# A two-layer decoder trunk: own places for each activation form, another row order in the last two output tiles, and two interleaved pairs

## The chip, the cores and the metric

The kernel runs on one core of a Trainium2 chip. TensorE (PE) does the matrix products, ScalarE (ACT) and VectorE (DVE) split, scale and gate, GpSimd (POOL) does small jobs and issues the accumulating loads, SyncE (SP) issues all other DMAs. The metric is the device time of one execution in microseconds, as the median of several runs.

## The reference, cut to what matters

512 positions, 2048 channels, two layers and a final norm, all in float32:

```python
def shortconv_layer(h, w_in, conv_w, w_out):
    gate_b, gate_c, u, z = jnp.split(h @ w_in, 4, axis=-1)
    y = gate_b * causal_depthwise_conv(gate_c * u, conv_w)
    return (y * jax.nn.silu(z)) @ w_out

def reference(...):
    h = x
    h = h + hybrid_layer(rmsnorm(h, norm_w[0]), ...)     # DeltaNet and windowed attention heads
    h = h + shortconv_layer(rmsnorm(h, norm_w[1]), ...)  # w_in: 2048 x 12288, w_out: 3072 x 2048
    return rmsnorm(h, final_norm_w)
```

The hybrid layer ends in an output projection of 3072 rows (24 tiles of 128, called rows 0 to 23 here) to 2048 columns (16 tiles). Its sum with x is h1, which the second layer normalizes, projects and gates.

## The kernel before

Activations stand with channels on the 128 partitions and the 512 positions along the free axis. Every float32 operand is split into a high and a low part, `hi` (a rounded copy, made by ACT) and `lo` (the difference, made by DVE), and each product is three matmuls: hi x hi, hi x lo, lo x hi (`mm3`). Weights come from DRAM in blocks of 128 x 8 x 128 (512 KB) and are split the same way (`load_split`, `split_w`).

**First output projection.** Each of its 16 output tiles m runs over the 24 split tiles `ys[k]`. Those of k < 16 lie in the pool `xp` (32 places of 128 x 512, under one tag, x), those of k from 16 in the pool `yd`. The last two tiles (14 and 15) run side by side over the three chunks of 8 rows in the order 0, 1, 2. `made(m)` adds the residual, writes h1 to DRAM (`H1d`), squares it into `ssq` for the norm and, for some m, scales it by the norm's weight (`scaled`) and makes the forms.

**Forms.** The second layer's input projection multiplies by Strassen's scheme in Winograd's form: the channels are halved (even and odd tiles 2j and 2j + 1) and the positions too, and each pair of output tiles takes 7 products of 8 steps j, with 256 positions a step. So seven combinations of h1 are needed, "forms" 0 to 6, each with eight tiles j, and each tile holds hi and lo. `forms` makes all seven for one j with 7 ACT copies and 11 DVE operations. Their 56 places are the 24 of the pool `x2p`, then the 32 of x as the `ys` leave them, handed out in the order in which `form` is called. For j 0 to 2 and j 7 the forms are made straight from h1; for j 3 to 6 `hr` tiles are read back from `H1d` (8 reads, through two places, which the squares `sq1` share by tag).

**Pairs.** `pair` makes two output tiles (of 96) from four quarters of the weights. Its products come in the order of the forms 0, 5, 6, 4, 1, 2, 3, into the banks acc, sb, sc, sb, acc, sb, sc. Raw blocks have eight places: two in `wp`, and six in the pool `w4`, which lies where `yd` lay. Each channel block c takes two pairs: C and u, then a gate and a causal convolution, then z and B, then the silu gate; the tiles cc, cu, cz and cb have six places under the tag ct. y of a block goes to DRAM (`Y2d`).

**Second output projection.** After the last pair the 24 tiles y come back from `Y2d` as `yl`, through the same six ct places, and are split by `split_y` into the places x (c < 16) and x2p (the others). 16 output tiles follow, and the final norm.

**Order.** The order of TensorE's instructions is that of the program. Side work (norms, heads) is a set of generators in `Flow`, put between matmuls when their due time in planned microseconds has come: the norm of the second layer (`rstd_task`) is due 5.0 after the last two tiles and a step of a product counts 0.36. On the other engines and in SP's queue a planner sets the order when the program is built, by program order as priority and by readiness in a simulated time; weight loads are marked as more urgent by `SPLIT_AHEAD`. In the run each engine keeps that order.

Of the kernel before, what the change touches and what calls it, by code (L numbers as in the profile page):

```python
# [7 lines left out]
F32 = mybir.dt.float32  # L8
F32R = mybir.dt.float32r
AF = mybir.ActivationFunctionType  # L10
ALU = mybir.AluOpType
# [19 lines left out]
NMT2 = 4 * NCH  # L31
NX2 = 24
NJ1 = 3
NRAW = 6
SPLIT_AHEAD = 600


# [37 lines left out]
def hybrid_trunk(ctx: ExitStack, tc: tile.TileContext, xT, w1, w1o, w2, w2o, nw, dcw, scw, hp, dnw, cst, msk, rope,  # L75
# [119 lines left out]

    def split_x(pool, tag, bufs, src, k, layer):
        hi = pool.tile([P, T], F32R, name="x_hi", tag=tag, bufs=bufs)
        lo = pool.tile([P, T], F32R, name="x_lo", tag=tag, bufs=bufs)
        A.activation(hi, src, AF.Copy, scale=nw_sb[:, layer, k:k + 1])
        V.scalar_tensor_tensor(lo, src, nw_sb[:, layer, k:k + 1], hi.bitcast(F32), op0=ALU.mult, op1=ALU.subtract)  # L200
        return hi, lo
# [3 lines left out]
    with tc.tile_pool(name="ini", bufs=3) as ini:  # L205
# [11 lines left out]
        for k in range(KT):  # L217
            xr = ini.tile([P, T], F32, name="xr", bufs=4)
            SP.dma_start(xr, xT[:, k, :])
            if k in (0, 1, 2, 4, 8, 12):  # L220
                k0, n = k, {0: 1, 1: 1, 2: 2}.get(k, 4)
                ws = [load_split(ini, w1[m][:, k:k + n, :], n, 4, 6, "i") for m in mts]
            xs1.append(split_x(xp, "x", 32, xr, k, 0))
            sq = ini.tile([P, T], F32, name="sq")
            A.activation(sq, xr, AF.Square)
            G.tensor_tensor(ssq, ssq, sq, op=ALU.add)
            for acc, (hi, lo) in zip(accs[:3 if k < 12 else 2], ws):
                mm3(acc, hi[:, k - k0, :], lo[:, k - k0, :], xs1[k], k == 0, k == KT - 1)
# [341 lines left out]
    with tc.tile_pool(name="dn", bufs=2, side="right") as dn:  # L570
# [165 lines left out]

        PX, PYD = (xp, "x", 32), (yd, "yd", 17)
        ys = [None] * KO

        def split_ready():  # L740
            for i, yt in enumerate(ytiles):
                if ys[i] is None and yt is not None:
                    ys[i] = split_y(PX if i < 16 else PYD, yt)

# [16 lines left out]
    rd2 = []  # L761
    slots = iter([(x2p, "x2", NX2)] * NX2 + [(xp, "x", 32)] * 32)
    fm = [[None] * NJ for _ in range(7)]

    def form(i, j, src):
        pool, tag, bufs = next(slots)
        t = pool.tile([P, 2, H], F32R, name="fm", tag=tag, bufs=bufs)
        A.activation(t[:, 0, :], src, AF.Copy)
        V.tensor_tensor(t[:, 1, :], src, t[:, 0, :].bitcast(F32), op=ALU.subtract)  # L769
        fm[i][j] = (t[:, 0, :], t[:, 1, :])  # L770

    def forms(pool, j, he, ho):
        e1, e2, o1, o2 = he[:, 0:H], he[:, H:T], ho[:, 0:H], ho[:, H:T]
        form(0, j, e1)
        fa, fb = (pool.tile([P, H], F32, name=n) for n in ("fa", "fb"))
        V.tensor_tensor(fa, e1, e2, op=ALU.subtract)
        V.scalar_tensor_tensor(fb, fa, -1.0, o2, op0=ALU.mult, op1=ALU.subtract)
        form(5, j, fb)
        form(4, j, fa)
        fc, fd = (pool.tile([P, H], F32, name=n) for n in ("fa", "fb"))  # L780
        V.tensor_tensor(fc, e2, o2, op=ALU.subtract)
        form(6, j, fc)
        form(1, j, o1)
        form(2, j, o2)
        V.tensor_tensor(fd, o1, fb, op=ALU.add)
        form(3, j, fd)

    with tc.tile_pool(name="op1", bufs=2, side="right") as op1:
# [8 lines left out]
        def made(m, acc, rx):  # L797
            h1 = rx
            V.tensor_tensor(h1, acc, rx, op=ALU.add)
            if m < 2 * NJ1 or m >= KT - 2:  # L800
                scaled(m, h1)
                if m % 2:
                    forms(op1, m // 2, hs[m - 1], hs[m])
            SP.dma_start(H1d[m], h1)
            sq = op1.tile([P, T], F32, name="sq1", tag="hr")
            A.activation(sq, h1, AF.Square)
            V.tensor_tensor(ssq, ssq, sq, op=ALU.add)

        def residual(m):
# [9 lines left out]
        accs = [new_acc() for _ in last]  # L819
        for c in range(KO // CK):  # L820
            with tc.high_priority(offset=SPLIT_AHEAD):
                ws = [load_split(wp, w1o[m][:, c * CK:(c + 1) * CK, :], CK) for m in last]
            for i in range(CK):
                k = c * CK + i
                flow.poll()
                for acc, (hi, lo) in zip(accs, ws):
                    mm3(acc, hi[:, i, :], lo[:, i, :], ys[k], k == 0, k == KO - 1)
        for j in range(NJ1, NJ - 1):
            for m in (2 * j, 2 * j + 1):
                hr = op1.tile([P, T], F32, name="hr", tag="hr")  # L830
                SP.dma_start(hr, H1d[m])
                scaled(m, hr)
            forms(op1, j, hs[2 * j], hs[2 * j + 1])
        for m, acc, rx in zip(last, accs, rxs):
# [4 lines left out]
    with tc.tile_pool(name="w4", bufs=1) as w4, tc.tile_pool(name="sc", bufs=1, side="right") as sc:  # L839
# [15 lines left out]

        def product(w, f, o, first):
            hi, lo = w
            o = o[:, 0:H]
            for j in range(NJ):
                flow.poll()  # L860
# [5 lines left out]

        def pair(wa, wb, c1, c2):
            with tc.high_priority(offset=SPLIT_AHEAD):
# [9 lines left out]
            with tc.high_priority(offset=SPLIT_AHEAD):  # L878
                w = split_w(q11)
            product(w, 0, a, True)  # L880
            a1 = sc.tile([P, H], F32, name="a1", bufs=2)
            A.activation(a1, a[:, 0:H], AF.Copy)
            with tc.high_priority(offset=SPLIT_AHEAD):
                V.tensor_tensor(q11, q11, s1, op=ALU.add)
                w = split_w(q11)
            product(w, 5, b, True)
            e = sc.tile([P, H], F32, name="e", bufs=2)
            V.tensor_tensor(e, b[:, 0:H], a1, op=ALU.add)
            with tc.high_priority(offset=SPLIT_AHEAD):
                w = split_w(s3)  # L890
            product(w, 6, c, True)
            with tc.high_priority(offset=SPLIT_AHEAD):
# [19 lines left out]
        def ctile(w=T):  # L912
            return sc.tile([P, w], F32, name="ct", tag="ct", bufs=6)

        rbc2 = sc.tile([P, T], F32, name="rbc2")
        for c in range(NCH):
            cc, cu = ctile(), ctile(T + 2)
            G.memset(cu[:, 0:2], 0.0)
            u = cu[:, 2:T + 2]
            pair(w2[4 * c], w2[4 * c + 1], cc, u)  # L920
            if c == 0:
# [7 lines left out]
            V.tensor_tensor(cc, cc, rbc, op=ALU.mult)  # L929
            cz, cb = ctile(), ctile()  # L930
            pair(w2[4 * c + 2], w2[4 * c + 3], cz, cb)
            V.tensor_tensor(cz, cz, rbc, op=ALU.mult)
# [6 lines left out]
            if c < NCH - 1:  # L939
                SP.dma_start(Y2d[c], yt)  # L940
        ys = [None] * NCH
        for c in range(NCH):
            if c < NCH - 1:
                yl = sc.tile([P, T], F32, name="yl", tag="ct", bufs=6)
                SP.dma_start(yl, Y2d[c])
            else:
                yl = yt
            ys[c] = split_y(PX if c < 16 else (x2p, "x2", NX2), yl)

# [128 lines left out]
```

## Time and profile before

| what | value |
|---|---|
| median of 3 runs | 2817.7 us (2816.68 to 2822.33) |
| profiled execution, own time | 2821.6 us |
| its span, first to last instruction | 2819.8 us |
| TensorE busy | 2774.8 us, 98% of the span |
| DVE, ACT, POOL busy | 64%, 39%, 6% |
| mean granted TensorE clock | 0.992 of full speed |

Busy shares are averages over the whole span. "SPq" is the queue of DMA issues on SP; a time shown for it runs from the first to the last issue of a merged entry. A granted clock of 1.00 is 2.4 GHz, of 0.5 is 1.2 GHz.

### The profile page before, as it was taken

Reading aid. Unit: us, or ns where it says so; the run is one execution under the profiler, and the core shown is the slowest. Engines: PE = TensorE matmul, PEld = TensorE weight load, DVE = VectorE, ACT = ScalarE, POOL = GpSimd, SP = SyncE. Lnnn points to the kernel's source line nnn. Section 1 sums busy time; section 2 is a strip of 40 time slices with the busy share of each in tenths; the row PEclk is TensorE's granted clock in tenths of the full one; section 3 lists DMA queues with packets and bytes.
Section 4 is the critical chain, followed back from the end, with each engine's and each line's share of the span. In section 5 each row is a group of like instructions: output and inputs, shape, how many; then the busy total and the mean of one; then the engine's idle time right before and its main releaser. Section 6 shows DMA issues by size and latency. Waiting matters only on the chain.

```text
span 2819.8 us, 41852 instructions
## 1 busy us (share of the span) xinstructions
PE 2774.8 (98%) x16648; PEld 2463.6 (87%) x16648; DVE 1798.9 (64%) x2707; ACT 1091.6 (39%) x1803; POOL 160.6 (6%) x226
## 2 busy tenths in 40 slices
PE   8999999999999999999999899999999999999998
PEld 6888888888887888888887899999999999997887
DVE  7766999555445655665334677777777777774223
ACT  5443444444432323234323444444444444443221
POOL 3110000000000000000000100000000000000000
PEclk9999999999999999999999999999999999999999
DMA  5655223322224333333444767776677676754333
GB/s 170 183 169 186 90 87 127 111 88 86 94 86 127 124 105 110 115 113 112 127 127 135 217 181 200 186 204 182 190 191 197 187 191 188 194 164 141 114 112 112
DMA packets 163059, 410.58 MB, mean 146 GB/s; under 512 B 41184, under 2 KB 55776, under 8 KB 162608
## 3 DMA queue, kind: packets, MB, share of 16 engines
q1 hardware_dynamic: 149040, 357.57, 39.4%
q0 software_dynamic: 13824, 50.34, 10.1%
q8 instruction: 131, 2.15, 0.3%
q14 instruction: 64, 0.52, 0.1%
HBM read 373.44 MB, written 34.41 MB: 145 GB/s over the span
## 4 chain that ended last, share of the span: by engine, by line
PE 93%; DVE 3%; DMA 2%; issue 1%; ACT 1%; SPq 0%; DVEq 0%; POOL 0%; ACTq 0%; POOLq 0%
PE acc L151 17%; PE acc L153 17%; PE acc L152 17%; PE sb L862 5%; PE sb L864 5%; PE sb L863 5%; PE sc L862 3%; PE sc L864 3%; PE acc L862 3%; PE acc L864 3%; PE sc L863 3%; PE acc L863 3%; PE p L96 2%; DMA w_raw<-in_w_dram 1%; DVE w_lo L146 1%
## 5 line engine op out<-in xcount | busy, mean ns | idle before, releaser
L151 PE MATMUL acc<-x_hi,w_hi 128*128 128x512 f32 x1536 | 622.5, 405 | 1.6 <-DVE cv_raw L319 1.6
L153 PE MATMUL acc<-x_hi,w_lo 128*128 128x512 f32 x1536 | 602.3, 392 | 5.1 <-DVE w_lo L146 5.1
L152 PE MATMUL acc<-x_lo,w_hi 128*128 128x512 f32 x1536 | 600.6, 391 | 0.5 <-DVE x_lo L200 0.3
L144 ACT ACTIVATE w_hi<-w_raw 128x1024 fp32r<-128x1024 f32 (+2 forms) x302 | 308.9, 1024 | 683.9 <-PE acc L152 513.9
L851 ACT ACTIVATE w_hi<-w_raw 128x1024 fp32r<-128x1024 f32 x336 | 356.3, 1061 | 559.2 <-PE acc L863 165.8
L146 DVE TENSOR_TENSOR w_lo<-w_raw,w_hi 128x1024 fp32r<-128x1024 f32 (+2 forms) x302 | 363.6, 1206 | 315.1 <-ACT w_hi L144 314.4
L853 DVE TENSOR_TENSOR w_lo<-w_raw,w_hi 128x1024 fp32r<-128x1024 f32 x336 | 411.0, 1224 | 160.9 <-ACT w_hi L851 159.0
L153 PEld LDWEIGHTS acc<-x_hi,w_lo 128*128 128x128 f32 x1536 | 289.2, 188 | 69.6 <-DVE w_lo L146 7.2
L151 PEld LDWEIGHTS acc<-x_hi,w_hi 128*128 128x128 f32 x1536 | 290.1, 189 | 57.4 <-DVE cv_raw L319 1.8
L152 PEld LDWEIGHTS acc<-x_lo,w_hi 128*128 128x128 f32 x1536 | 290.3, 189 | 55.8 <-DVE x_lo L200 1.8
L862 PE MATMUL sb<-fm,w_hi 128*128 128x256 f32 x1152 | 325.9, 283 | 0.0
L864 PE MATMUL sb<-fm,w_lo 128*128 128x256 f32 x1152 | 325.2, 282 | 0.0
L863 PE MATMUL sb<-fm,w_hi 128*128 128x256 f32 x1152 | 324.5, 282 | 0.0
L151 PE MATMUL acc<-y_hi,w_hi 128*128 128x512 f32 (+1 forms) x792 | 307.6, 388 | 4.8 <-ACT y_hi L732 3.2
L152 PE MATMUL acc<-y_lo,w_hi 128*128 128x512 f32 (+1 forms) x792 | 305.7, 386 | 3.5 <-DVE y_lo L734 3.5
L153 PE MATMUL acc<-y_hi,w_lo 128*128 128x512 f32 (+1 forms) x792 | 305.8, 386 | 1.2 <-DVE w_lo L146 1.2
L862 PE MATMUL sc<-fm,w_hi 128*128 128x256 f32 x768 | 218.0, 284 | 5.5 <-ACT w_hi L851 5.5
L862 PEld LDWEIGHTS sb<-fm,w_hi 128*128 128x128 f32 x1152 | 219.7, 191 | 0.0
L863 PEld LDWEIGHTS sb<-fm,w_hi 128*128 128x128 f32 x1152 | 218.9, 190 | 0.0
L864 PEld LDWEIGHTS sb<-fm,w_lo 128*128 128x128 f32 x1152 | 218.5, 190 | 0.0
L864 PE MATMUL sc<-fm,w_lo 128*128 128x256 f32 x768 | 217.5, 283 | 0.5 <-DVE w_lo L853 0.5
L863 PE MATMUL acc<-fm,w_hi 128*128 128x256 f32 x768 | 216.0, 281 | 1.3 <-DVE fm L769 1.3
(241 smaller groups left out, 4322.5 us busy)
## 6 DMA issues: line engine op xcount, KB each, us to landing
w_raw<-in_w_dram SPq DMA_DIRECT2D x428, 512.0 KB, 4.4
w_raw<-in_w_dram POOLq DMA_DIRECT2D x96, 512.0 KB, 7.1
w_raw<-in_w1o_dram SPq DMA_DIRECT2D x48, 512.0 KB, 3.6
w_raw<-in_w2o_dram SPq DMA_DIRECT2D x48, 512.0 KB, 3.6
Y2d<-y SPq DMA_DIRECT2D x23, 256.0 KB, 5.3
yl<-Y2d SPq DMA_DIRECT2D x23, 256.0 KB, 4.4
xr<-in_xT_dram SPq DMA_DIRECT2D x16, 256.0 KB, 4.3
KQd<-kq SPq DMA_DIRECT2D x8, 512.0 KB, 5.1
```

Of the source, the lines that this page charges most:

```text
L96: PE.matmul(o, lhsT, rhs, start=start, stop=stop)
L144: A.activation(hi, raw, AF.Copy)
L146: V.tensor_sub(lo, raw, hi.bitcast(F32))
L151: PE.matmul(acc, hi, xh, start=first, stop=False)
L152: PE.matmul(acc, hi, xl, start=False, stop=False)
L153: PE.matmul(acc, lo, xh, start=False, stop=last)
L851: A.activation(hi, src, AF.Copy)
L853: V.tensor_sub(lo, src, hi.bitcast(F32))
L862: PE.matmul(o, hi[:, j, :], xh, start=first and j == 0, stop=False, skip_group_check=not first)
L863: PE.matmul(o, hi[:, j, :], xl, start=False, stop=False, skip_group_check=not first)
L864: PE.matmul(o, lo[:, j, :], xh, start=False, stop=j == NJ - 1, skip_group_check=not first)
```

## The change

- The pool `xp` now has four tags x0 to x3 of eight places, for rows 0-3, 4-7, 8-11 and 12-15. Each form has eight places of its own: forms 0, 5, 6 in `x2p` (f0, f1, f2), form 4 in x0, 1 in x1, 2 in x2, 3 in x3.
- The last two output tiles read the chunks in the order 2, 0, 1.
- `made` makes forms 0, 5 and 6 of every j straight from h1 (all seven for j 7). Forms 4 and 1, and then forms 2 and 3, come in two passes over j 0 to 6, and each pass reads all 14 tiles back (28 reads). For tiles 14 and 15 the write of h1 stands behind the square.
- `pair` is a generator that stops after three products. In the first block it does them with steps 0 to 6 of all three first and step 7 of all three after, and the second pair does its own first three before the first pair goes on. Other blocks keep their order.
- ct has four places, `yl` three of its own. y of block c is split into the places of forms 0, 5, 6, 4, 1, 2, four blocks to each.

```diff
-    def split_x(pool, tag, bufs, src, k, layer):
-        hi = pool.tile([P, T], F32R, name="x_hi", tag=tag, bufs=bufs)
-        lo = pool.tile([P, T], F32R, name="x_lo", tag=tag, bufs=bufs)
+    def split_x(src, k, layer):
+        hi, lo = (xp.tile([P, T], F32R, name=n, tag=f"x{k // 4}", bufs=8) for n in ("x_hi", "x_lo"))
         A.activation(hi, src, AF.Copy, scale=nw_sb[:, layer, k:k + 1])
         V.scalar_tensor_tensor(lo, src, nw_sb[:, layer, k:k + 1], hi.bitcast(F32), op0=ALU.mult, op1=ALU.subtract)
...
-        PX, PYD = (xp, "x", 32), (yd, "yd", 17)
+        PYD = (yd, "yd", 17)
         ys = [None] * KO
 
         def split_ready():
             for i, yt in enumerate(ytiles):
                 if ys[i] is None and yt is not None:
-                    ys[i] = split_y(PX if i < 16 else PYD, yt)
+                    ys[i] = split_y((xp, f"x{i // 4}", 8) if i < 16 else PYD, yt)
...
-    slots = iter([(x2p, "x2", NX2)] * NX2 + [(xp, "x", 32)] * 32)
+    EARLY, LATE = (0, 5, 6), (4, 1, 2, 3)
+    homes = [(x2p, "f0"), (xp, "x1"), (xp, "x2"), (xp, "x3"), (xp, "x0"), (x2p, "f1"), (x2p, "f2")]
     fm = [[None] * NJ for _ in range(7)]
 
     def form(i, j, src):
-        pool, tag, bufs = next(slots)
-        t = pool.tile([P, 2, H], F32R, name="fm", tag=tag, bufs=bufs)
+        pool, tag = homes[i]
+        t = pool.tile([P, 2, H], F32R, name="fm", tag=tag, bufs=NJ)
         A.activation(t[:, 0, :], src, AF.Copy)
         V.tensor_tensor(t[:, 1, :], src, t[:, 0, :].bitcast(F32), op=ALU.subtract)
         fm[i][j] = (t[:, 0, :], t[:, 1, :])
 
-    def forms(pool, j, he, ho):
+    def forms(pool, j, he, ho, which):
         e1, e2, o1, o2 = he[:, 0:H], he[:, H:T], ho[:, 0:H], ho[:, H:T]
-        form(0, j, e1)
+        if 0 in which:
+            form(0, j, e1)
         fa, fb = (pool.tile([P, H], F32, name=n) for n in ("fa", "fb"))
         V.tensor_tensor(fa, e1, e2, op=ALU.subtract)
-        V.scalar_tensor_tensor(fb, fa, -1.0, o2, op0=ALU.mult, op1=ALU.subtract)
-        form(5, j, fb)
-        form(4, j, fa)
-        fc, fd = (pool.tile([P, H], F32, name=n) for n in ("fa", "fb"))
-        V.tensor_tensor(fc, e2, o2, op=ALU.subtract)
-        form(6, j, fc)
-        form(1, j, o1)
-        form(2, j, o2)
-        V.tensor_tensor(fd, o1, fb, op=ALU.add)
-        form(3, j, fd)
+        if 5 in which or 3 in which:
+            V.scalar_tensor_tensor(fb, fa, -1.0, o2, op0=ALU.mult, op1=ALU.subtract)
+        if 5 in which:
+            form(5, j, fb)
+        if 6 in which:
+            fc = pool.tile([P, H], F32, name="fa")
+            V.tensor_tensor(fc, e2, o2, op=ALU.subtract)
+            form(6, j, fc)
+        if 4 in which:
+            form(4, j, fa)
+        if 1 in which:
+            form(1, j, o1)
+        if 2 in which:
+            form(2, j, o2)
+        if 3 in which:
+            fd = pool.tile([P, H], F32, name="fb")
+            V.tensor_tensor(fd, o1, fb, op=ALU.add)
+            form(3, j, fd)
...
         def made(m, acc, rx):
             h1 = rx
             V.tensor_tensor(h1, acc, rx, op=ALU.add)
-            if m < 2 * NJ1 or m >= KT - 2:
-                scaled(m, h1)
-                if m % 2:
-                    forms(op1, m // 2, hs[m - 1], hs[m])
-            SP.dma_start(H1d[m], h1)
+            scaled(m, h1)
+            if m % 2:
+                forms(op1, m // 2, hs[m - 1], hs[m], EARLY if m < KT - 1 else EARLY + LATE)
+            if m < KT - 2:
+                SP.dma_start(H1d[m], h1)
             sq = op1.tile([P, T], F32, name="sq1", tag="hr")
             A.activation(sq, h1, AF.Square)
             V.tensor_tensor(ssq, ssq, sq, op=ALU.add)
+            if m >= KT - 2:
+                SP.dma_start(H1d[m], h1)
...
-        for c in range(KO // CK):
+        order = (2, 0, 1)
+        for c in order:
             with tc.high_priority(offset=SPLIT_AHEAD):
                 ws = [load_split(wp, w1o[m][:, c * CK:(c + 1) * CK, :], CK) for m in last]
             for i in range(CK):
                 k = c * CK + i
                 flow.poll()
                 for acc, (hi, lo) in zip(accs, ws):
-                    mm3(acc, hi[:, i, :], lo[:, i, :], ys[k], k == 0, k == KO - 1)
-        for j in range(NJ1, NJ - 1):
-            for m in (2 * j, 2 * j + 1):
-                hr = op1.tile([P, T], F32, name="hr", tag="hr")
-                SP.dma_start(hr, H1d[m])
-                scaled(m, hr)
-            forms(op1, j, hs[2 * j], hs[2 * j + 1])
+                    mm3(acc, hi[:, i, :], lo[:, i, :], ys[k], c == order[0] and i == 0, c == order[-1] and i == CK - 1)
+        for which in (LATE[:2], LATE[2:]):
+            for j in range(NJ - 1):
+                for m in (2 * j, 2 * j + 1):
+                    hr = op1.tile([P, T], F32, name="hr", tag="hr")
+                    SP.dma_start(hr, H1d[m])
+                    scaled(m, hr)
+                forms(op1, j, hs[2 * j], hs[2 * j + 1], which)
...
-        def product(w, f, o, first):
+        def product(w, f, o, first, js=range(NJ)):
             hi, lo = w
             o = o[:, 0:H]
-            for j in range(NJ):
+            for j in js:
...
-        def pair(wa, wb, c1, c2):
+        def pair(wa, wb, c1, c2, early=False):
...
             a, b, c = new_acc(), bank("sb"), bank("sc")
             with tc.high_priority(offset=SPLIT_AHEAD):
-                w = split_w(q11)
-            product(w, 0, a, True)
-            a1 = sc.tile([P, H], F32, name="a1", bufs=2)
-            A.activation(a1, a[:, 0:H], AF.Copy)
+                wa0 = split_w(q11)
+            if not early:
+                product(wa0, 0, a, True)
+                a1 = sc.tile([P, H], F32, name="a1", bufs=2)
+                A.activation(a1, a[:, 0:H], AF.Copy)
             with tc.high_priority(offset=SPLIT_AHEAD):
                 V.tensor_tensor(q11, q11, s1, op=ALU.add)
-                w = split_w(q11)
-            product(w, 5, b, True)
-            e = sc.tile([P, H], F32, name="e", bufs=2)
-            V.tensor_tensor(e, b[:, 0:H], a1, op=ALU.add)
+                wb0 = split_w(q11)
+            if not early:
+                product(wb0, 5, b, True)
+                e = sc.tile([P, H], F32, name="e", bufs=2)
+                V.tensor_tensor(e, b[:, 0:H], a1, op=ALU.add)
             with tc.high_priority(offset=SPLIT_AHEAD):
-                w = split_w(s3)
-            product(w, 6, c, True)
+                wc0 = split_w(s3)
+            if not early:
+                product(wc0, 6, c, True)
+            else:
+                for js in (range(NJ - 1), range(NJ - 1, NJ)):
+                    for w, f, o in ((wa0, 0, a), (wb0, 5, b), (wc0, 6, c)):
+                        product(w, f, o, True, js)
+                a1 = sc.tile([P, H], F32, name="a1", bufs=2)
+                A.activation(a1, a[:, 0:H], AF.Copy)
+                e = sc.tile([P, H], F32, name="e", bufs=2)
+                V.tensor_tensor(e, b[:, 0:H], a1, op=ALU.add)
+            yield
...
         def ctile(w=T):
-            return sc.tile([P, w], F32, name="ct", tag="ct", bufs=6)
+            return sc.tile([P, w], F32, name="ct", tag="ct", bufs=CT)
 
         rbc2 = sc.tile([P, T], F32, name="rbc2")
         for c in range(NCH):
             cc, cu = ctile(), ctile(T + 2)
             G.memset(cu[:, 0:2], 0.0)
             u = cu[:, 2:T + 2]
-            pair(w2[4 * c], w2[4 * c + 1], cc, u)
+            cz, cb = ctile(), ctile()
+            p1 = pair(w2[4 * c], w2[4 * c + 1], cc, u, c == 0)
+            p2 = pair(w2[4 * c + 2], w2[4 * c + 3], cz, cb)
+            next(p1)
+            if c == 0:
+                next(p2)
+            for _ in p1:
+                raise AssertionError
...
-            cz, cb = ctile(), ctile()
-            pair(w2[4 * c + 2], w2[4 * c + 3], cz, cb)
+            for i, _ in enumerate(p2):
+                assert c and not i
...
         ys = [None] * NCH
+        FREED = (0, 5, 6, 4, 1, 2)
         for c in range(NCH):
             if c < NCH - 1:
-                yl = sc.tile([P, T], F32, name="yl", tag="ct", bufs=6)
+                yl = sc.tile([P, T], F32, name="yl", bufs=3)
                 SP.dma_start(yl, Y2d[c])
             else:
                 yl = yt
-            ys[c] = split_y(PX if c < 16 else (x2p, "x2", NX2), yl)
+            ys[c] = split_y(homes[FREED[c // 4]] + (NJ,), yl)
 
     with tc.tile_pool(name="op2", bufs=2, side="right") as op2:
         ssq = rsx.tile([P, T], F32, name="ssq2")
```

## Rows read from the trace of the kernel before

**Rows 1.** Stretches: span, then busy time (instructions) by engine, clock, DMA share, GB/s.
```profile
core 0: us, PE busy (x) PEld busy (x) DVE busy (x) ACT busy (x) POOL busy (x), PEclk, DMA share, GB/s
1400.00:1470.00 70.00, 70.00 (x310) 57.95 (x310) 20.95 (x23) 15.89 (x17) 0.00 (x0) 1.00 0.42 133
1470.00:1540.00 70.00, 67.25 (x288) 54.52 (x286) 32.89 (x62) 27.22 (x50) 1.06 (x1) 0.98 0.46 143
1540.00:1610.00 70.00, 62.43 (x442) 59.80 (x443) 44.32 (x60) 26.70 (x37) 7.36 (x10) 0.93 0.69 192
1680.00:1750.00 70.00, 70.00 (x589) 70.00 (x589) 54.33 (x65) 30.18 (x37) 6.25 (x9) 1.00 0.73 197
2520.00:2590.00 70.00, 63.23 (x277) 49.08 (x276) 36.18 (x48) 29.23 (x42) 0.00 (x0) 0.95 0.54 173
```
**Rows 2.** TensorE's waits from 1545 to 1610: total us, times, longest.
```profile
PE sc L862 <- ACT w_hi L851: 5.5, 1, 5.5
```
**Rows 3.** The chain that ended last, 1490 to 1600: start, us, what.
```profile
1554.83 9.79 DMA w_raw<-in_w_dram
```
**Rows 4.** TensorE's timeline at the first join: start, us, instruction.
```profile
1549.96 0.28 PE L862 MATMUL acc<-fm,w_hi 128*128 128x256 f32 x1
...
1558.57 0.83 PE L96 MATMUL rs_ps<-cst_sb,ssq 128*128 128x128 f32 x6
...
1584.38 0.28 PE L862 MATMUL acc<-fm,w_hi 128*128 128x256 f32 x1
```
**Rows 5.** A stretch behind the idle time, columns as in rows 1.
```profile
1566.00:1575.00 9.00, 8.54 (x50) 8.24 (x51) 6.30 (x7) 3.70 (x5) 0.95 (x2) 0.67 0.94 269
```
**Rows 6.** TensorE's timeline: first matmuls of the second output projection's tiles 0 and 1.
```profile
2526.57 0.40 PE L151 MATMUL acc<-y_hi,w_hi 128*128 128x512 f32 x1
...
2556.42 0.39 PE L151 MATMUL acc<-y_hi,w_hi 128*128 128x512 f32 x1
```
**Rows 7.** The tile yl, 2490 to 2560: ns min/median/max, first and last start.
```profile
L732 ACT ACTIVATE y_hi<-yl x23: 612/630/634, 2522.2 to 2551.0; 128x512 fp32r<-128x512 f32 x23
L734 DVE TENSOR_TENSOR y_lo<-yl,y_hi x23: 684/689/695, 2523.2 to 2551.7; 128x512 fp32r<-128x512 f32 x23
...
DMA to landing us min/median/max: 2.7/4.4/6.7
```
**Rows 8.** Timeline of SP, DVE and ACT around the ct places, 2498 to 2534.
```profile
2498.74 0.86 SPq L945 DMA_DIRECT2D yl<-Y2d  x2
...
2513.59 0.32 SPq L945 DMA_DIRECT2D yl<-Y2d  x1
...
2512.79 0.74 DVE L928 SCALAR_TENSOR_TENSOR ct<-ct,scw_sb 128x512 f32<-128x512 f32 x1
...
2521.93 0.37 ACT L901 ACTIVATE ct<-acc 128x256 f32<-128x256 f32 x1
...
2533.15 0.68 DVE L938 SCALAR_TENSOR_TENSOR y<-ct,gzs 128x512 f32<-128x512 f32 x1
```
**Rows 9.** The tile hr, 1505 to 1540, columns as in rows 7.
```profile
L831 SPq DMA_DIRECT2D hr<-H1d x8: 319/323/557, 1513.3 to 1529.3; - x8
L795 ACT ACTIVATE hs<-hr,nw_sb x8: 705/717/725, 1516.4 to 1533.5; 128x512 f32<-128x512 f32 x8
...
DMA to landing us min/median/max: 2.5/3.0/4.7
```
**Rows 10.** The tile hs, 1505 to 1560, columns as in rows 7.
```profile
L769 DVE TENSOR_TENSOR fm<-hs,fm x15: 417/420/427, 1517.6 to 1556.1; 128x256 fp32r<-128x256 f32 x15
```
**Rows 11.** Timeline of SP, ACT and DVE around the hr places, 1512 to 1515.
```profile
1513.31 0.56 SPq L831 DMA_DIRECT2D hr<-H1d  x1
...
1512.96 0.62 ACT L806 ACTIVATE sq<-rx 128x512 f32<-128x512 f32 x1
...
1514.22 0.69 DVE L807 TENSOR_TENSOR ssq<-ssq,sq 128x512 f32<-128x512 f32 x1
```
**Rows 12.** The page's groups: weight splits of the pairs, count, busy us, mean ns.
```profile
L851 ACT ACTIVATE w_hi<-w_raw 128x1024 fp32r<-128x1024 f32 x336 | 356.3, 1061 | 559.2 <-PE acc L863 165.8
...
L853 DVE TENSOR_TENSOR w_lo<-w_raw,w_hi 128x1024 fp32r<-128x1024 f32 x336 | 411.0, 1224 | 160.9 <-ACT w_hi L851 159.0
```

More of the change, by code (lines that the diff above doesn't have):

```diff
@@ L31 @@
 NMT2 = 4 * NCH
-NX2 = 24
-NJ1 = 3
 NRAW = 6
 SPLIT_AHEAD = 600
+CT = 4
 class Flow:
@@ L222, in hybrid_trunk @@
                 ws = [load_split(ini, w1[m][:, k:k + n, :], n, 4, 6, "i") for m in mts]
-            xs1.append(split_x(xp, "x", 32, xr, k, 0))
+            xs1.append(split_x(xr, k, 0))
             sq = ini.tile([P, T], F32, name="sq")
```

## The prediction

> **What bounds the kernel now.** The table of stretches comes first [rows 1]. The reader is to see that TensorE is busy for every microsecond of a quiet stretch, of the output projection (1400 to 1470 us: 310 instructions, 0.226 us each) as of the pairs (1680 to 1750: 589, 0.119 us each). Nothing that shortens DVE, ACT or DMA inside a stage moves the time. Only two joins fall short: 67.25 and 62.43 of 70 us where the first output projection hands over to the pairs, 63.23 where the last pair hands over to the second output projection.
>
> The waits name the first join's cause [rows 2]: the product into sc waited 5.5 us for the split of its weights, and the chain shows the load behind it, 9.79 us in one piece [rows 3]. Starts of matmuls give the full price [rows 4]: the first pair runs from 1549.96 to 1584.38, 34.4 us. It has 7 products of 8 steps, a step is three matmuls or 0.357 us, so 20.0 us are work; the norm's two groups of 8 small matmuls (six of one group take 0.83 us) are another 2.2. Some 12.2 us are lost, part of them at a clock of 0.67 of full speed behind the idle time [rows 5].
>
> At the second join the first tile of the second output projection takes from 2526.57 to 2556.42 [rows 6], 29.9 us for 72 matmuls that need 16.3 at 0.226: 13.6 us lost. There y comes late: its 23 splits on ACT all start between 2522.2 and 2551.0 [rows 7].
>
> **Part one: own places, second join.** Before, a y split waits for places that forms of all seven kinds hold. After, y 0 to 3 take the places of form 0, which the last pair is through with after its first product, and so on in the order of the products. The last pair begins 56 x 0.357 = 20.0 us ahead of 2526.6, at 2506.6, so y 0 can be split at some 2507 to 2508 and not at 2522.2. What limits y then is its loads, which get three places of their own where they shared six. A load holds a place for its landing (2.7 at least, 4.4 in the median), ACT 0.63 and DVE 0.69 [rows 7] and its issue, 0.32 [rows 8]: 4.3 to 6.0 us, with three places 1.45 to 2.0 us per y. Three are there early; the load of y 3 goes out at about 2508.4, that of y 22 nineteen later, so y 22 is split at 2540.3 to 2552.4. TensorE wants it at 2526.6 + 22 x 0.68 = 2541.6. So nothing to 10.8 us of the 13.6 stay lost. I take the middle, 1.75, because the first loads meet few others and the later ones meet the weights of the projection: y 22 at 2546.9, 5.3 us late, a gain of **8.3 us** (2.8 to 13.6).
>
> CT = 4 I cost at nothing. The old tiles are read until the chain of a channel block ends (L938, at 2533.83 [rows 8]), 7.3 us after its last matmul; the new cu is first filled after four products of the next pair, 11.4 us. The cover is 4.1 us. Only the small memset on POOL meets the wait, and behind it on POOL stand the accumulating loads of a later pair; without that cover each of 23 blocks would pay its wait.
>
> **Part two: the order 2, 0, 1.** The places of rows 16 to 23 come free 96 matmuls (21.7 us) earlier, so the first pair's raw blocks load while TensorE still works, and the 9.79 us load [rows 3] leaves the path. Places x0 to x3 come free later than before, within the last 21.7 us; forms 4, 1, 2 and 3 wait for them.
>
> **Part three: forms in passes.** Forms 0, 5 and 6 move into the projection: two scalings of 0.72 [rows 9], three ACT copies and six DVE operations of 0.42 [rows 10] per two tiles of 33 us, beside 21 us of DVE and 16 of ACT in 70 [rows 1]: hidden. The price is in the re-reads. They go from 8 to 28 (two passes over 14 tiles, 20 x 256 KB more on SP) through two places, hr, which the squares of `made` share. The trace shows how places are given out. The first re-read went out at 1513.31, right behind the square of tile 13 that takes a place at 1512.96 [rows 11], though its data had been in DRAM for long. Likewise two yl loads went out from 2498.74 and the third only at 2513.59 [rows 8], when cu's last reader ended (2513.53): four of six places were held for cc, cu, cz and cb, though cz was first written at 2521.93. I read that places go in program order. The squares of tiles 14 and 15 stand behind all 28 re-reads in the program, hence in time.
>
> How long are 28? One load holds its place for a landing of 3.0 (2.5 to 4.7), a scaling of 0.72 [rows 9] and an issue of 0.32: with two places 2.02 us each by the median, 1.77 by the fastest. The eight of before took 16.0 us from first to last issue [rows 9], 2.29 each, with 11 DVE operations per two tiles where a pass now has 3 or 5. I take 2.02: last issue 1513.3 + 27 x 2.02 = 1567.8, landed 1570.8, scaled 1571.5, squared (0.62) and added (0.69) [rows 11] at 1572.8. TensorE comes to the norm's matmuls after 14 steps of the first pair, at about 1551, and everything on it stands behind them. Then remain 10 steps of pair one's early three, 24 of pair two's and 32 of pair one's rest, 66 x 0.357 = 23.6; the norm, 2.2; 3.0 at low clock, as before (9 us at 0.67 [rows 5]); and 1.6 because three splits are now held together and pair two's first (ACT 1.06, DVE 1.22 [rows 12]) starts when two steps, 0.7 us, are left to hide it. Pair one, with three products of pair two, ends at 1572.8 + 30.4 = 1603.2. Before, the same work ends at 1584.4 + 24 x 0.357 = 1593.0: **10.2 us lost** (3.0 at 1.77 us per load, 17.5 at 2.29).
>
> By the Trainium skill (DMA: Bandwidth & Descriptors, Anatomy of one DMA — SWDGE (gpsimd) path) a transfer costs 2.0 us plus its bytes over 436 GB/s, a fit for the software path; for 256 KB that is an estimated 2.6 where the rows have 3.0, and the loss would be 4.5.
>
> **The sum.** 10.2 - 8.3 = +1.9 us on the profiled execution of 2821.6 us (span 2819.8). That execution lies 3.9 above the median of the runs, 2817.7; carried over, **2819.6**, its own range 2810 to 2831.
>
> **Rivals.** *The squares are not held up*: places go to whoever is ready, and nothing waits for re-reads until product 2 of pair one. The last two tiles begin at about 1512 [rows 11] and need 144 x 0.226 = 32.5; with a little of today's stalls they end at 1546. 48 steps, the norm and the split bring TensorE to 1567, products 4 and 1 to 1572.7; the last form is ready at 1571.5 + 5 x 0.42 = 1573.6, in time for its step. Pair one ends at 1578.4, a gain of 14.6, with the second join 22.9: **2794.8**. For it: DVE and ACT have room [rows 1]. Against it: the places [rows 8, 11].
>
> *Half of it*: the squares come through, but splits stand in order behind late re-reads on ACT and DVE. The first join comes out even: **2809.4**.
>
> *Re-reads and weights collide.* The raw blocks of both pairs, 512 KB each, now load in the same 50 us. At the landing that yl has under load, 4.4 [rows 7], a re-read costs 2.72 us, the last is issued at 1586.7 and the squares are added at 1593.1, 20.3 us later than in the sum: 30.5 lost less 8.3, **2839.9**; from 2.2 us per load on it is slower by over 0.2%. Against it: the 3.0 [rows 9] was itself measured beside weight loads. The Trainium skill (DMA: Bandwidth & Descriptors, Issuing engines are not separate DMA queues) lets the DMAs of all issuing engines run on the same 16 DMA engines; by that prefetch and re-reads do collide, and no row here gives the rate.
>
> **How the numbers follow.** 0.2% (5.6 us) is about what a measurement of this kernel can tell from no change. Forecast 0.50 (0.08 faster, 0.28 same, 0.14 slower), squares free 0.27 (faster), half 0.10 (0.07 faster, 0.03 same), collision 0.13 (slower). Faster 0.42, same 0.31, slower 0.27. The range leaves out the outer parts of the free and the colliding case: 2793 to 2834.
>
> **What would show it.** Right: 28 re-reads, the last issued near 1568; TensorE idle some 20 us ahead of rs_ps, released by DVE's ssq; no wait for sc's weights; y splits from about 2508 and the second projection's first tile in some 22 us. Wrong: rs_ps by 1553; re-reads at under 1.6 us or over 2.5; y splits that still begin at 2522, which with three places would cost and not gain.

## The result, and the profile after

The changed kernel takes 2853.4 us (median of 4 runs, 2852.1 to 2854.5), the kernel before 2817.6 beside it: ratio 1.0124, 95% interval 1.0106 to 1.0141, slower by 35.8 us. That is outside the range of 2793 to 2834, and far from the forecast of 2819.6, which was no clear change. The profiled execution of after is 2852.1 us (span 2850.4), 30.5 over the profiled one of before, which lay 3.9 above its median.

TensorE's waits from 1500 to 1640, in order of size (total us, times, longest):

```profile
PE rs_ps L95 <- DVE ssq L815: 32.4, 1, 32.4
PE sb L874 <- ACT w_hi L863: 4.3, 1, 4.3
```

The 5.5 us for sc's weights [rows 2] are gone. In their place stands one wait of 32.4 us, of the norm's matmuls for the sum of squares. The stretches show what it does to TensorE (columns as in [rows 1]):

```profile
1470.00:1540.00 70.00, 66.20 (x290) 53.86 (x288) 24.20 (x36) 23.20 (x35) 1.94 (x2) 1.00 0.53 170
1540.00:1610.00 70.00, 29.83 (x161) 26.37 (x162) 35.46 (x74) 34.80 (x65) 3.80 (x5) 0.71 0.52 146
1556.00:1596.00 40.00, 4.93 (x21) 4.43 (x21) 21.39 (x50) 24.51 (x47) 0.87 (x1) 0.55 0.54 158
2520.00:2590.00 70.00, 65.36 (x413) 57.30 (x412) 51.26 (x68) 35.09 (x49) 0.86 (x1) 0.93 0.54 167
```

From 1540 to 1610 TensorE is busy 29.8 of 70 us, where it was 62.4 [rows 1]; from 1556 to 1596 it is nearly idle at a granted clock of 0.55. No engine replaces it as the bound there: DVE and ACT are busy for 21 and 25 of 40 us. Starts of matmuls give the price:

```profile
1551.46 0.28 PE L874 MATMUL acc<-fm,w_hi 128*128 128x256 f32 x1
...
1596.26 2.08 PE L95 MATMUL rs_ps<-cst_sb,ssq 128*128 128x128 f32 x8 [32.43 <-DVE ssq L815]
...
1626.71 0.28 PE L874 MATMUL sb<-fm,w_hi 128*128 128x256 f32 x1
```

Pair one with three products of pair two runs from 1551.46 to 1626.71, 75.3 us. Before, the same work took 1593.0 - 1550.0 = 43.0 [rows 4]. **32.2 us are lost at the first join**, where 10.2 were forecast.

What the sum of squares waited for is in the chain that ended last. These are its pieces on the re-reads' data and behind them (start, us, what):

```profile
1530.57 15.91 DMA hr<-H1d
...
1547.31 8.32 DMA hr<-H1d
...
1590.37 2.48 DMA hr<-H1d
1592.87 0.73 ACT hs L803
...
1595.61 0.61 DVE ssq L815
1596.26 2.08 PE rs_ps L95 x8
```

SyncE's timeline says when the loads went out (a row is a run of issues from its first start to its last end):

```profile
1516.61 8.54 SPq L843 DMA_DIRECT2D hr<-H1d  x5
1525.20 0.42 SPq L885 DMA_DIRECT2D w_raw<-in_w_dram  x1
...
1529.92 0.60 SPq L882 DMA_DIRECT2D w_raw<-in_w_dram  x1
1530.57 2.66 SPq L843 DMA_DIRECT2D hr<-H1d  x2
...
1547.31 9.42 SPq L843 DMA_DIRECT2D hr<-H1d  x3
...
1562.26 28.43 SPq L843 DMA_DIRECT2D hr<-H1d  x15
```

Here are two rates. The last 15 re-reads take 2.0 us each, the forecast's value. But from 1525.2 to 1530.5 SyncE issues eight raw weight blocks (seven of the pairs, one of the last output tiles), and then only seven re-reads go out in the 31.7 us from 1530.57 to 1562.26, one of them landing after 15.9 us. In the same stretch POOL issues four accumulating loads of 512 KB (1530.74 to 1546.42). The DMA view of 1530 to 1562 sets SyncE's queue beside POOL's (packets, MB, share of the 16 engines' time):

```profile
q1 hardware_dynamic: 2364, 6.27, 55.8%
q0 software_dynamic: 576, 2.10, 34.3%
```

Per MB, POOL's loads took nearly twice the engines' time of SyncE's queue, in which the re-reads stand. The tile hr in all:

```profile
L843 SPq DMA_DIRECT2D hr<-H1d x28: 319/320/652, 1514.3 to 1590.4; - x28
...
DMA to landing us min/median/max: 2.5/2.9/15.9
```

First to last issue is 76.1 us, 2.82 per load; the median landing, 2.9, is as before [rows 9] and hides it.

The second join, tile yl:

```profile
L730 ACT ACTIVATE y_hi<-yl x23: 612/629/633, 2539.6 to 2582.1; 128x512 fp32r<-128x512 f32 x23
...
L977 SPq DMA_DIRECT2D yl<-Y2d x20: 319/320/1745, 2542.2 to 2579.5; - x20
...
DMA to landing us min/median/max: 2.6/3.4/4.6
```

The splits start 18.9 us ahead of the projection's first matmul (2558.5), where they started 4.4 ahead [rows 6, 7]. The 20 loads take 1.96 us each. Tile 0 goes from 2558.53 to 2585.78, 27.3 us where it took 29.9: a gain of 2.6, not 8.3. Its stretch (columns as in [rows 1]):

```profile
2558.53:2585.78 27.25, 22.61 (x75) 15.36 (x73) 16.22 (x24) 12.23 (x19) 0.00 (x0) 0.84 0.66 220
```

TensorE waits 4.6 us for y. It is busy for 22.6 us with work of 16.3, at a mean granted clock of 0.84 (0.89 in the same tile before): the clock costs more here than the waits.

### The profile page after: what moved, and what is told of

It reads as the page before. It is cut to its first block, busy times and chain, and to the rows that moved or that the text cites. A ratio compares the mean times of both kernels' runs of the same rounds, so it can differ in the third digit from the quotient of the medians.

```text
span 2850.4 us, 41963 instructions
## 1 busy us (share of the span) xinstructions
PE 2773.1 (97%) x16648; PEld 2460.9 (86%) x16648; DVE 1806.2 (63%) x2728; ACT 1110.9 (39%) x1831; POOL 161.1 (6%) x226
## 4 chain that ended last, share of the span: by engine, by line
PE 91%; DMA 4%; DVE 2%; ACT 1%; issue 1%; SPq 0%; DVEq 0%; POOL 0%; ACTq 0%
PE acc L150 17%; PE acc L152 17%; PE acc L151 17%; PE sb L874 5%; PE sb L876 5%; PE sb L875 5%; PE sc L874 3%; PE sc L876 3%; PE sc L875 3%; PE acc L874 3%; PE acc L876 3%; PE acc L875 3%; DMA hr<-H1d 2%; PE p L95 2%; PE o_ps L95 1%
## 5 line engine op out<-in xcount | busy, mean ns | idle before, releaser
L876 PE MATMUL acc<-fm,w_lo 128*128 128x256 f32 x768 | 215.9, 281 | 0.8 <-DVE w_lo L865 0.8
```

Source lines behind the costliest of these rows:

```text
L876: PE.matmul(o, lo[:, j, :], xh, start=False, stop=j == NJ - 1, skip_group_check=not first)
```

## The experiments

The theory after this reading: the norm waits because tiles 14 and 15 stand in the program behind 28 re-reads, and these are slow because the raw weight blocks crowd them out. Its rivals: TensorE is held by something else that comes equally late (the late forms, the weights); or the collision is not what sets the re-reads' time. Times below are medians, gains are against 2853.4; the kernel before ran beside each, at 2817.5 to 2819.9. For gains below 9 us the interval of the ratio to before still overlaps that of the changed kernel (at 8.7 only just): 2 us are not told apart from nothing, 5 to 6 are likely and not certain.

**Free the squares' places.**

```
sq = op1.tile([P, T], F32, name="sq1", tag="hr") if m < KT - 2 else bank("sqm")
```

> Edit: the squares of tiles 14 and 15 go to a bank of PSUM that is free here, not to a place of hr; all else as in the changed kernel (2853.4 us). Theory (everything of tiles 14 and 15 stands in the program behind 28 re-reads that take 78 us from first to last, so hs as well as the squares): the 32 us wait of rs_ps goes, but the scaled copies of tiles 14 and 15 still wait for a place of hs behind the re-reads, so TensorE stops 7 steps later, at the last step of product 0, until some 1595 us. Gain 1 to 5 us: 2848 to 2852. Rival (the squares' places alone hold the join up): the join runs through until products 4 and 1; gain about 25 us, 2828.

2848.0 us, a gain of 5.4. TensorE's largest wait is now this one:

```profile
PE acc L874 <- ACT fm L767: 26.4, 1, 26.4
```

The norm is free and the stop moved, as the theory had it. The rival's 25 us are not there.

**Free the scaled copies too.**

```
hz = op1.tile([P, T], F32, name="hz", bufs=1)
...
scaled(m, h1, {KT - 2: hz, KT - 1: acc}.get(m))   # and one place each for fa, fb
```

> Edit: as in the run before, and the scaled copies of tiles 14 and 15 get places of their own as well (2 KB freed by letting forms 6 and 3 reuse fa and fb). Theory: the norm's matmuls and forms 0, 5, 6 of the last pair of tiles come through by some 1556 us, 48 steps and the norm run without a stop to about 1575, and the next stop is the first late form, until the last pass (forms 2 and 3) is through at 1595; pair one's remaining 32 steps then end at some 1600 to 1607 and not at 1626.6. Gain 20 to 27 us: 2826 to 2834. Rival (TensorE is held up by the re-reads' load on DMA, that is by late weights, and not by places): weights of pair two come as late as before and the gain is under 8 us.

2851.4, a gain of 2.0: my figure was wrong, and the rival's "under 8" held. Its reason holds in part at most: a wait for the weights of product 5 grew from 4.3 us to 7.8, but the largest wait names forms:

```profile
PE sb L874 <- ACT fm L767: 28.7, 1, 28.7
```

It ends when the forms of the last two tiles come, at 1607, after the last re-read (1602.3 scaled): they now took turns with the late forms for fa and fb. Each place that is freed hands the wait to the next.

**Finish tiles 14 and 15 between the passes.**

```
for which in (LATE[:2], LATE[2:]):
    for j in range(NJ - 1 if which == LATE[:2] else NJ):
        ...
    if which == LATE[:2]:
        for m, acc, rx in zip(last, accs, rxs):
            made(m, acc, rx)
```

> Edit: in the program, tiles 14 and 15 are finished between the two passes (their add, scaled copies, forms 0, 5, 6, 4 and 1, squares), and the second pass reads all 16 tiles again for forms 2 and 3. Theory (places are given out in program order, so whatever stands behind a re-read in the program waits for it; with two places freed the wait only moved to forms through fa and fb): tiles 14 and 15 now stand behind 14 re-reads and not 28, the norm comes at about 1565 to 1572 us, TensorE has 26 us of work from there, and the second pass is through at about 1600, in time or some us late for products 2 and 3. Gain 15 to 24 us on 2853.4: 2829 to 2838. Rival (the late forms' own arrival sets the end whatever the program order, which is why freed places gained 2 to 5 us): gain under 5 us, 2848 or more.

2847.3, a gain of 6.1; the theory's 15 to 24 failed, the rival's "under 5" is near. The norm's wait fell to 3.6 us, but the last of the re-reads (30 here) landed at 1607.4, and a long wait followed:

```profile
PE sb L875 <- DVE e L915: 14.7, 1, 14.7
```

The name is that of a small sum, e, for which product 4 of the first pair waits. DVE came to it at 1611.2, behind the forms of the last re-read. So program order decided which matmul stops, and the re-reads' end still set when it goes on. Whether products 4 and 1, whose forms were made in the first pass, would have run earlier with e ahead of those forms on DVE was not tried.

**Half the re-reads.**

```
for which in (LATE,):
```

> Edit: the late forms of a pair of tiles are made in one pass, so that 14 tiles are read again and not 28; order and places as in the changed kernel. Theory (the number of re-reads times what one costs sets the time of the squares): the last re-read goes out near 1566 us and not at 1590, squares at 1570 to 1573, gain 20 to 26 us: 2827 to 2833. Rival (what sets the end is the stretch of 30 us in which 512 KB loads crowd the re-reads out, or places of x0 to x3 that come free late, not their number): the 14 end nearly where the 28 did, gain under 8 us.

2825.1, a gain of 28.3, more than forecast. The number of re-reads is the lever. The 14 still took 46.4 us, 3.6 each:

```profile
L843 SPq DMA_DIRECT2D hr<-H1d x14: 319/320/453, 1518.9 to 1565.3; - x14
...
DMA to landing us min/median/max: 2.5/3.3/15.9
```

Two landings on the chain that ended last hold half of it:

```profile
1535.06 15.92 DMA hr<-H1d
...
1551.81 7.04 DMA hr<-H1d
```

**Move the weights away, with 28 and with 14 re-reads.**

```
order = (0, 1, 2)
```

> Edit: the last two tiles read rows 0 to 23 in their old order; all else as in the changed kernel. The places of rows 16 to 23, and with them four of the raw weight blocks, then come free some 20 us later. Theory (the weights loaded ahead crowd out the re-reads: some 8 in 30 us, at landings up to 15.9 us, against 2.0 us each in quiet): re-reads run at about 2 us each until 1550 and more of them are done when the weights start; the squares come some 10 us earlier, but the pair's weights come later, so the join gains 3 to 15 us, 2838 to 2850, and landings over 6 us shift to after 1545. Rival (no collision: 28 re-reads take what they take): squares as late as before and weights later too, no gain or a loss of up to 10 us: 2853 to 2863.

> Edit: one pass (14 re-reads) together with the order 0, 1, 2. Theory (the re-reads lose some 25 us to the loads of weights that start when the places of rows 16 to 23 come free; with 14 of them and the old order nearly all are through before that): at 2.0 us each the 14 end by some 1548 us, the norm is not held up, and what is left is the late weights of the first pair, 5 to 10 us as in the kernel before: 2812 to 2822. Rival (order 2, 0, 1 pays in one pass, because the weights then set the end): worse than one pass alone, 2828 or more.

With 28: 2851.2, a gain of 2.2, just under the forecast. SyncE's timeline has both rates again:

```profile
1545.29 10.63 SPq L843 DMA_DIRECT2D hr<-H1d  x6
1555.97 0.42 SPq L885 DMA_DIRECT2D w_raw<-in_w_dram  x1
...
1559.59 1.20 SPq L843 DMA_DIRECT2D hr<-H1d  x2
...
1575.38 1.88 SPq L843 DMA_DIRECT2D hr<-H1d  x2
```

Until the row of weight blocks begins at 1556.0, 20 re-reads go out, 2.06 us apart, close to the forecast's 2.02. Behind it the 15 us landing follows, at 1559.6, still inside the re-reads, and the last eight take until 1584.9. With 14 they are through before that row of blocks starts:

```profile
L843 SPq DMA_DIRECT2D hr<-H1d x14: 319/320/427, 1516.5 to 1545.1; - x14
...
DMA to landing us min/median/max: 2.6/3.3/4.8
```

28.6 us where 14 took 46.4 in the order 2, 0, 1, with the same loads: **the collision costs 14 re-reads 17.8 us**. The order also moves the time at which x0 to x3 come free, but the landings of 15.92 and 7.04 us alone are 16.4 over two of the median 3.3, which leaves little for places. The total hardly moved all the same, 2824.5 to 2825.1, because a wait of 8.6 us for sc's weights came back, as in [rows 2]. The order 2, 0, 1 saves that wait and pays it in re-reads.

**Another queue.**

```
A.dma_start(hr, H1d[m])
```

> Edit: the 28 re-reads are issued by ScalarE and not by SyncE, so that they stand in another DMA queue than the raw weight blocks. Theory (a re-read that lands after 15.9 us stood behind 4 MB of weight blocks in SyncE's queue; 4 MB in 15.9 us is 264 GB/s, what the DMA moved there): landings stay under 6 us, the stretch of 28 shrinks by 12 to 25 us, gain 10 to 22 us: 2831 to 2843. Rival (all queues share the same 16 DMA engines, and a re-read gets no more of them from another queue): landings up to 10 us and more, gain under 5 us, or a loss, because ScalarE issues them in its own order.

2854.9, no gain. The longest landing fell to 9.3 us, so part of the 15.9 was the place in SyncE's queue; but 28 took 76.4 us as before:

```profile
L843 ACTq DMA_DIRECT2D hr<-H1d x28: 326/326/351, 1518.3 to 1594.7; - x28
...
DMA to landing us min/median/max: 2.6/3.0/9.3
```

From 1530 to 1562 the DMA share is 0.97 here at 286 GB/s (0.90 and 262 in the changed kernel). This fits a lack of share: the DMA engines are busy, and another queue gives the re-reads no more of them. It is not the whole of it, since ScalarE's own order held them up too: one went out at 1557.73, though its place was free from 1554.1, behind a weight split that waited for its block. By the Trainium skill (DMA: Bandwidth & Descriptors, Issuing engines are not separate DMA queues) the DMAs of all issuing engines run on the same 16 DMA engines; the 76.4 us against 76.1 agree.

**The second join alone.**

```
yl = ... bufs=3) if c < 6 else w4.tile([P, T], F32, name="yl", tag="w_raw4", bufs=NRAW)
```

> Edit: the loads of y 6 to 22 go to the six raw weight places that the last pair has done with, beside the three places of their own; the first join is as in the changed kernel. Theory (three places set the rate of the y loads, 1.96 us each, and TensorE wants one each 0.68 us): with nine places the loads run at some 1.0 us each, the first tile of the second projection goes through in 16 to 20 us and not 27; gain 6 to 11 us on 2853.4: 2842 to 2847. Rival (the loads meet the weights of the second projection on the DMA and keep their rate, or the raw places come free late): gain under 3 us.

2844.6, a gain of 8.7. Busy TensorE in the stretch of the second join rises from 65.36 to 69.22:

```profile
2520.00:2590.00 70.00, 69.22 (x463) 63.55 (x462) 53.95 (x72) 37.56 (x52) 0.86 (x1) 1.00 0.59 181
```

The loads went out from 2534.1 to 2567.4, 1.75 us each and not the 1.0 that I expected: they gained by starting 8 us earlier, not by their rate. Three places were the limit in that the fourth load had to wait for the first split. TensorE's 4.6 us of waits for y are gone, and in this stretch the granted clock stays at 1.00 where it was 0.93.

**The start.** In three profiles with x in four groups, the first norm's matmuls, which ran at 47.4 us before, ran at 50.4, 55.9 and 54.0. So the grouping was tried by itself, once added to the kernel before and once taken from the changed one.

```
hi, lo = (xp.tile([P, T], F32R, name=n, tag=f"x{k // 4}", bufs=8) for n in ("x_hi", "x_lo"))   # in before
hi, lo = (xp.tile([P, T], F32R, name=n, tag="x", bufs=32) for n in ("x_hi", "x_lo"))           # in after
```

> Edit: the kernel before, with nothing of the change but one thing: the 32 places of x are four groups of 8 (x0 to x3) and not one of 32. The order in which the engines take their work then differs in the first 60 us (splits of x and of weights stand in pairs and don't alternate) and in a few later places. Theory (part of the loss is made there: the first matmuls of the norm ran at 47.4 us in the profile of before, and at 50.4, 55.9 and 54.0 in three profiles with the groups): slower than before by 3 to 8 us, 2820 to 2826, and rs_ps of the start at 50 us or later. Rival (the start varies from execution to execution by as much, and the groups cost nothing): within 2 us of before.

> Edit: the changed kernel with the 32 places of x as one group again; forms 4, 1, 2 and 3 and the y of the second projection take places from that one group; the work of the start stands in the order of the kernel before. Theory (as in the run before): faster than the changed kernel by 3 to 8 us, 2845 to 2850. Rival (the groups cost nothing at the start, or one group delays forms and y by as much as it saves): within 2 us of 2853.4.

2823.9, which is 6.1 us slower than before (ratio 1.0019, interval 1.0010 to 1.0028), and 2847.7, which is 5.7 faster than the changed kernel. The first interval lies clear of 1; the second gain is likely and not certain. DVE's splits at the start alternate in the kernel before (first rows); with the groups alone added (second rows) they stand in pairs, and the norm's matmuls start 3.7 us later:

```profile
14.88 0.74 DVE L200 SCALAR_TENSOR_TENSOR x_lo<-xr,nw_sb,x_hi 128x512 fp32r<-128x512 f32 x1
15.55 0.42 DVE L146 TENSOR_TENSOR w_lo<-w_raw,w_hi 128x256 fp32r<-128x256 f32 x1
15.88 0.75 DVE L200 SCALAR_TENSOR_TENSOR x_lo<-xr,nw_sb,x_hi 128x512 fp32r<-128x512 f32 x1
16.54 0.42 DVE L146 TENSOR_TENSOR w_lo<-w_raw,w_hi 128x256 fp32r<-128x256 f32 x1
```

```profile
13.22 0.48 DVE L146 TENSOR_TENSOR w_lo<-w_raw,w_hi 128x128 fp32r<-128x128 f32 x2
13.62 2.43 DVE L199 SCALAR_TENSOR_TENSOR x_lo<-xr,nw_sb,x_hi 128x512 fp32r<-128x512 f32 x2
15.97 1.84 DVE L146 TENSOR_TENSOR w_lo<-w_raw,w_hi 128x256 fp32r<-128x256 f32 x2
```

```profile
51.15 0.89 PE rs_ps L96 x8
```

The delay lasts. The first output projection's first add, before and with the groups alone added:

```profile
1316.12 0.69 DVE L799 TENSOR_TENSOR rx<-acc,rx 128x512 f32<-128x512 f32 x1 [2.50 <-PE acc L152]
```

```profile
1319.67 0.69 DVE L798 TENSOR_TENSOR rx<-acc,rx 128x512 f32<-128x512 f32 x1 [2.46 <-DMA rx<-in_xT_dram]
```

In the eleven profiles with four groups this add comes 0.8 (the changed kernel) to 8.0 us later than in that of before; in the four other profiles with one group (the second run here and three below) between 1.4 earlier and 0.7 later. So the start varies, and the groups cost time there. That all of the 6.1 arises there is not shown. Why the grouping changes the order was not settled.

**Together.** One pass with the raw places for y; then also order 0, 1, 2 and x in one group; then that version with the order 2, 0, 1 again, and with the pairs one after the other as before (`p1 = pair(...)` without `c == 0`, no `next(p2)`).

> Edit: one pass over 14 tiles, and the loads of y 6 to 22 in the raw weight places; order 2, 0, 1. Theory (the two are in different joins and add): 2825.1 - 9 = 2816, within 3. Rival (the second join's gain depends on how late the first one ends, or on DMA work that the first leaves behind): 2820 or more.

> Edit: one pass, order 0, 1, 2, the loads of y 6 to 22 in the raw weight places, and x in one group. Theory (three separate places: 2824.5 with one pass and the old order, less 9 at the second join, less 3 to 8 at the start): 2808 to 2813, faster than both kernels. Rival (forms 4, 1, 2 and 3 in one group wait for places in turn and y 12 to 22 of the second projection wait for the last product): 2815 or more.

> Edit: the fastest version so far (2809.2 us: one pass, order 0, 1, 2, y in raw places, x in one group), with the order 2, 0, 1 again. Theory (the order 2, 0, 1 saves the wait for the first pair's weights, 8 to 9 us, and loses nearly as much because the weights then crowd out 14 re-reads, 46 us for them and not 29): 2808 to 2813, no clear difference. Rival (with y and x out of the way one of the two sets the end alone): 4 us or more apart.

> Edit: the fastest version so far, without the three products of each of the first two pairs ahead of the rest: the pairs run one after the other as in the kernel before. Theory (with the norm no longer held up, 48 steps ahead of the rest give the late forms and the weights of products 4, 1, 2 and 3 some 17 us more; but the late forms are through by 1557 us here, and six splits of weights are then wanted at once): within 4 us of 2809.2. Rival (the early products are what hides the weights): slower by 6 us or more.

2816.1, as summed, level with the kernel before (ratio 0.9992, interval 0.9983 to 1.0001). 2809.2 (ratio to before 0.9966, interval 0.9952 to 0.9979): faster than both kernels. The order 2, 0, 1 in it: 2813.2 (0.9977, 0.9966 to 0.9987). That is 4.0 apart, where the rival begins, but the intervals overlap: no clear difference, as the theory said. Without the early products: 2804.3 (0.9942, 0.9928 to 0.9955), the fastest. The theory's 4 us either way is just missed, and the rival had it slower. Two waits of TensorE, first of the version with the early products, then of the one without:

```profile
PE sc L874 <- ACT w_hi L863: 9.0, 1, 9.0
```

```profile
PE sc L874 <- ACT w_hi L863: 5.5, 1, 5.5
```

The same block of weights is late in both (a load of 9.9 and of 9.8 us). With the early products TensorE comes to it after 14 steps and not 16, and three splits follow in a row; that this explains the longer wait is argued and not shown. From 1540 to 1610 TensorE is busy 57.9 us with them and 61.1 without. The two intervals against before just overlap, so the 6 us or so are likely and not certain.

## Why the prediction was wrong, step by step

**What bounds the kernel: right.** Nothing in a stage changed; the loss is at the first join and, unforeseen, at the start.

**Part one, second join: right mechanism, wrong size.** The splits came early, as said. "I take the middle, 1.75" was the term: with three places the loads took 1.96, near the slow end of 1.45 to 2.0, and the gain was 2.6 against 8.3. The rate makes 4.0 of the missing 5.7 (19 loads at 0.21); the rest stays open. The sum had no term for the clock: 0.84 in tile 0 with 4.6 us of waits left, and 1.00 in the run without them. That CT = 4 costs nothing was right: TensorE waits for nothing between 1620 and 2480.

**The start: a step that was left out.** The prediction costed the groups of x where their places come free and nowhere else. They also changed the order of the first 60 us; measured alone, the groups cost 6.1 us.

**Part two: half right.** The wait of 5.5 us for sc's weights went. That the early weights would meet the re-reads stood as a rival and not in the sum.

**Part three: the step that failed is "How long are 28?", "I take 2.02".** The order of events was right: squares behind all re-reads, TensorE idle ahead of rs_ps, released by DVE's ssq. So was what follows the squares: from the last add's end, 1596.2, to the end of pair one 30.5 us, where the sum had 30.4. What was wrong is the re-reads' rate, 2.82 us against 2.02, which put the last squares at 1596.2 and not 1572.8: 23.4 us. Of the 23.4 the rate makes 27 x 0.80 = 21.6; the first re-read was 1.0 later too. "Over 2.5" was the prediction's own sign of being wrong. The 2.02 came from eight re-reads [rows 9] with four single loads between them in 16 us, and was carried to a stretch into which the change itself puts eight blocks of 512 KB. The prediction had the rival's price, 2.72 us and 30.5 lost; the runs show 2.82 and 32.2. It was given 0.13 because the 3.0 us landing "was itself measured beside weight loads". The pair with 14 re-reads shows how different: 28.6 us without the blocks, 46.4 with them.

**The sum.** 32.2 - 2.6 and 0.8 of a later start make 30.4 between the two profiled executions, 30.5 measured; other differences, up to 1.8 us each, cancel. Between the medians it is 35.8; the profiled execution of before was 3.9 us above its median, that of after 1.2 below. The 6.1 of the groups should be part of the 35.8; in the profiled execution of after, by chance, only 0.8 us of it shows at the start, the least of the eleven profiles.

**The rival "the squares are not held up"** priced a wait that, once removed, uncovers the next: freeing the squares gave 5.4 us and not 25. The late forms arrive as late as the squares did, for the same reason.

## What to carry to other kernels

A landing time read in a quiet stretch does not hold for a stretch that the change fills with prefetch: add up the bytes that will be in flight there, and price small loads by the share that is left. When a wait has one visible cause, ask what arrives next behind it, and cut the work that all of them wait for (here 28 loads to 14) before freeing places one at a time. And when a change regroups buffers, compare the order of instructions everywhere, also far from the place that was meant.

## What the runs showed of the hardware that was not expected

A load of 256 KB, whose median landing over the 28 is 2.9 us, landed after 15.9 with eight blocks of 512 KB ahead of it in SyncE's queue, and a later one after 8.3, beside a ninth block (1541.55) and POOL's accumulating loads, at a DMA share of 0.90 and 262 GB/s. Issuing the re-reads from another engine cut the longest landing to 9.3 us and left the time of all 28 as it was (76.4 us against 76.1). The accumulating loads took 34.3% of the DMA engines' time for 2.10 MB, beside 55.8% for 6.27 MB on SyncE's queue.
